# Standing pairs of TensorE transposes side by side in a two-block kernel: token halves, hidden tiles, exponentials, normed heads, diagonals

## The chip, the cores and the metric

One core of a Trainium2 chip runs the whole program in one launch. The metric is the time of the program on the device in microseconds (us). TensorE multiplies matrices and also does the transposes, as products with the identity; VectorE (DVE) and ScalarE (ACT) copy, scale and apply functions; GpSimd (POOL) does a few small things; SyncE (SP) issues the transfers of the weights.

## The reference

256 tokens of width 1024 pass through two blocks, each of two or one layers, in float32. Cut to what matters:

```
first block, layer 0 and layer 1:
  proj = rmsnorm(h) @ w_in[l];  main, mq = proj[..., :768], proj[..., 768:]
  main_out = pool_mixer(main)                       # layer 0
  main_out = swa_sink_attention(q(main), k, v)      # layer 1, 12 query heads, window 128
  mk, mv   = halves of rmsnorm(mem) @ w_mem_kv[l]
  mem_out  = softmax(norm(mq) @ norm(mk).T / 8) @ mv    # 4 heads of 64, 256 memory rows
  h += concat(main_out, mem_out) @ w_out[l]
  h += relu(rmsnorm(h) @ w_up[l])**2 @ w_down[l]
second block (normed h -> x):
  gated linear recurrence over the tokens (queries, forget gates, values per head of 128)
  block attention over normed query and key heads
  both, gated, through an output projection
  h += (silu(x @ w_gate) * (x @ w_up)) @ w_down
```

## The kernel before, in words

**Tiling.** The 256 tokens are two tiles of 128 (`tt` is 0 or 1). A left operand of a product needs its contraction axis on the partitions, so whatever is normed, gated or squared per token is first transposed: `tr` (line 159) multiplies one 128x128 piece by the identity `ident` into a PSUM bank called `mm`. Four such pieces fill a bank of 128x512, so transposes come in groups of four (two where a group has only two pieces), and one or two copies by ACT and DVE take a bank out.

**Precision.** A large product is three TensorE products of rounded halves: a weight is cast by ACT to `wh` (line 242) and its remainder is made by DVE as `wl` (line 243); an activation becomes `xh` and `xl` (`split`, lines 366 to 383), or `yh` and `yl` for a hidden tile. The three are (wh, xh), (wl, xh), (wh, xl), each 128x512 or 128x256 columns wide, at line 152. Weights come by SP's queue into `raw` tiles and go through eight buffers of `wh` and `wl`.

**Order.** A planner written out by hand (class `Line`, lines 88 to 121) sets the order of the program. Each piece of work is a generator task with a rank; it yields a delay in modelled us, or an event, when it has to wait for another engine. `mm` and `tr` move the planner's clock on. At each step the planner runs the task of the lowest rank whose delay has passed. So a `yield 1.3` between two groups of transposes lets other tasks (mostly the large products) issue in between. A list scheduler behind it then places instructions by engine; TensorE carries them out in the order that results.

**The places that the change touches.**

- `Norm.into` (line 401) normalizes a token tile, transposes its two halves of 512 columns (`xn`), and splits them; the two halves are apart by a `yield`. `turned` (line 508) does the same for a tile `h` that is not normed first.
- In `mlp` (line 553) `up_one` makes a hidden block for one token tile and hands it to `turn(b, tt, y)` (line 564), which transposes it (`hid`): four pieces in the square-relu MLPs, two in the gated one (class `SiluGate`, line 637). `up_one` is used for the blocks at the start of an MLP, before the steady loop.
- `mem_attention` (line 867) has two exponentials tiles `me`, one for each row half of the array; `exp_T` (line 441) transposes one into a bank and copies it as `eT` (ACT, line 448), and the products with the memory's values `mv` follow.
- `on_q` and `diagonal` (lines 1228 and 1240) make the diagonal of the recurrence's score matrix: many 32x32 products of `qs` and `fK` into an `mm` bank, and a multiplication by DVE into `AI` (line 1246). The recurrence then goes on in levels (line 1249), each with a burst of small products of `fQ` and `fK`.
- `heads_proj` and `heads_T` (lines 1385 and 1370) norm four heads of 128 (`hn`), transpose them and copy them out.

Of the kernel before, what the change touches and what calls it, by code (L numbers as in the profile page):

```python
# [15 lines left out]
P = 128  # L16
# [25 lines left out]
def kernel(  # L42
# [340 lines left out]
    class Norm:  # L383
# [17 lines left out]
        def into(self, xs, tt, g, done):  # L401

            xn, lat = self.xn, 1.2
            if self.r is None:
                self.rstd()
                lat = 3.0
            else:
                xn = keep.tile([P, D], F32, tag="xn", name="xn", bufs=2)
            for c in range(2):
                V.tensor_scalar(xn[:, half(c)], self.src[:, half(c)], self.r, None, op0=ALU.mult)  # L410
            for c in range(2):
                yield lat
                split_T(xn[:, half(c)], xs, tt, 4 * c, 4, g[:, 4 * c:4 * c + 4])
                lat = 0.8
            done.at(2.0)
# [92 lines left out]
    def turned(xs, src, tt, g, done):  # L508

        for c in range(2):  # L510
            split_T(src[:, half(c)], xs, tt, 4 * c, 4, None if g is None else g[:, 4 * c:4 * c + 4])
            yield 1.3
        done.at(1.5)

# [38 lines left out]
    def mlp(key, xs, there, nb, ku, hidden, finish, ends=1):  # L553
# [9 lines left out]

        def turn(b, tt, y):
            yield 3.2
            split_T(y, hT[b], tt, 0, ku)
            hT_there[b, tt].at(5.1)

        def up_one(b, tt):
# [4 lines left out]
            yield from lin(ps, ktiles(xs, tt), W((key, "up", b)))  # L574
            line.add(-2, turn(b, tt, hidden(ps)))

# [290 lines left out]
    def mem_attention(l, q, xs, tt, q_there, done):  # L867
# [20 lines left out]
        for i, ps in enumerate(pss):  # L888
# [9 lines left out]
            for hp in range(2):  # L898
                scaled(e[i][:, hp, :], sm[:, 2 * i + hp:2 * i + hp + 1])
        yield 3.2  # L900
        eTs = []
        for i in range(2):
            eTs.append(exp_T([e[i][:, hp, tok(c)] for hp in range(2) for c in range(2)]))
            yield 1.5
        po = by128(mm_bank())
# [313 lines left out]
    def on_f(c, hs, ps):  # L1219
        A.activation(fF[c][:, hs, :], ps, AF.Sigmoid)  # L1220
        A.activation(fK[c][:, hs, :], ps, AF.Sigmoid, scale=-1.0)
        for i in range(hs.start, hs.stop):
# [3 lines left out]
            V.tensor_scalar(k, k, olb[:, hd:hd + 1], None, op0=ALU.mult)  # L1226

    def on_q(c, hs, ps):
        V.scalar_tensor_tensor(fQ[c][:, hs, :], ps, HG_SCALE, fF[c][:, hs, :], op0=ALU.mult, op1=ALU.mult)
        qs = b2([2, S], "qs")  # L1230
        A.activation(qs, ps, AF.Copy, scale=HG_SCALE)
        line.add(5, diagonal(c, hs, qs))

# [5 lines left out]

    def diagonal(c, hs, qs):  # L1240
        yield 1.5
        pd = mm_bank()[:, :128].rearrange("p (h t) -> p h t", t=32)
        for i in range(2):
            for tt in range(TT):
                quarters(pd[:, 2 * i + tt, :], fK[c][:, hs.start + i, tok(tt)], qs[:, i, tok(tt)], 32)
        V.tensor_tensor(AI[c][:, 2 * hs.start:2 * hs.stop, :], pd, own[:, None, :].to_broadcast([P, 4, 32]), ALU.mult)
        diag_done[c, hs.start].at(2.1)

# [42 lines left out]

    diag_done = {(c, j): Event() for c in range(2) for j in (0, 2)}
    A_there, hv_there = events(), events()
# [7 lines left out]
    def recurrence(c):  # L1301
        yield [diag_done[c, 0], diag_done[c, 2]]
        for m in (1, 2, 4, 8, 16, 32, 64):
# [65 lines left out]

    def heads_T(t, dst, scale, done):  # L1370

        y = head_norm(t, 4, P, b2([4, P], "hn"))
        yield 8.4
        pt = by128(mm_bank())
        for i in range(4):
            tr(pt[:, i, :], y[:, i, :])
        if scale is None:
            A.copy(dst, pt)
        else:
            A.activation(dst, pt, AF.Copy, scale=scale)  # L1380
        left[done] = left.get(done, 0) + 1
        if left[done] == 2:
            done.at(5.8)

    def heads_proj(key, c, tt, dst, scale, done):
        t = b2([4, P], "tm")
        A.copy(t, by128((yield from project((key, c), x2, tt))))
        line.add(9, heads_T(t, dst, scale, done))

# [209 lines left out]
```

## Time and profile before

| | |
|---|---|
| median of 3 runs | 1031.24 us (1030.45 to 1032.26) |
| the profiled execution, its own time | 1031.49 us |
| its span, first to last instruction | 1029.6 us |
| TensorE products busy | 1022.1 us, 99% |
| TensorE weight loads (beside the products) | 901.6 us, 88% |
| VectorE busy | 640.0 us, 62% |
| ScalarE busy | 565.4 us, 55% |
| granted TensorE clock, mean | 1.000 |

The span is what the profile's pages divide into; the execution's own time is 1.9 us longer, and the median of the runs shown is 0.25 us below that execution's time. The rows of a timeline give the start, the length, the engine, the line, the operation and the tiles (out<-in). A product's end in the trace is modelled, and successive products overlap, so the cost of a group on TensorE is read from starts: from the start of the last product before it to the start of the second one behind it, less the usual distance of the products.

### The profile page before, as it was taken

The page shows a single profiled execution, that of the slowest core. Times are in us where ns is not written, and L with a number is a line of the kernel's source. Part 1 is how long each engine was busy: PE and PEld are TensorE (multiplying, and loading weights), DVE is VectorE, ACT ScalarE, POOL GpSimd, SP SyncE. Part 2 cuts the span into 40 slices and gives each one's busy share as a digit, 9 for nine tenths or more (in the row PEclk, how much of TensorE's full clock was granted, in tenths as well). Part 3 has the DMA queues.
Part 4 walks back from the last instruction along what each step waited for, and adds up shares of the span by engine and source line. Part 5 has one row for each costly group of instructions (what it writes and reads, how often), then busy time and mean ns, then how long its engine had stood idle before and what let it go on. Part 6 is the DMA issues. An engine that isn't in the chain of part 4 may idle for free.

```text
span 1029.6 us, 18411 instructions
## 1 busy us (share of the span) xinstructions
PE 1022.1 (99%) x7353; PEld 901.6 (88%) x7353; DVE 640.0 (62%) x1002; ACT 565.4 (55%) x904; POOL 100.8 (10%) x143
## 2 busy tenths in 40 slices
PE   9999999999999999999999999999999999999998
PEld 8768999998876788899988988888999988999997
DVE  6976664565678765564576569847635766455553
ACT  6856544454678654444466455758744455444341
POOL 1524000000142000000000004330000000000000
PEclk9999999999999999999999999999999999999999
DMA  9854566556552269666557554334455566565741
GB/s 339 279 164 163 166 196 208 169 185 207 181 165 82 71 182 327 198 191 212 171 181 237 196 165 165 124 124 156 142 184 175 179 196 199 164 216 167 231 145 41
DMA packets 107765, 186.40 MB, mean 181 GB/s; under 512 B 6808, under 2 KB 31648, under 8 KB 107680
## 3 DMA queue, kind: packets, MB, share of 16 engines
q1 hardware_dynamic: 106160, 180.13, 53.8%
q0 software_dynamic: 1104, 4.80, 1.4%
q8 instruction: 57, 0.93, 0.4%
q10 hardware_dynamic: 416, 0.30, 0.1%
q14 instruction: 28, 0.23, 0.1%
HBM read 182.58 MB, written 2.63 MB: 180 GB/s over the span
## 4 chain that ended last, share of the span: by engine, by line
PE 94%; DVE 2%; DMA 2%; issue 1%; ACT 0%; ACTq 0%
PE acc L152 58%; PE mm L152 33%; PE mm L159 3%; DMA raw<-in_w_mem_kv_dram 1%; DVE wl L248 1%; DMA raw<-in_w_in_dram 1%; DMA raw_T<-in_xT_dram 0%; DVE wl L243 0%; DVE u L932 0%; DVE u L820 0%; DVE hs L427 0%; ACT xn L398 0%; DVE win L931 0%; ACT wh L247 0%; DVE win L927 0%
## 5 line engine op out<-in xcount | busy, mean ns | idle before, releaser
L243 DVE TENSOR_TENSOR wl<-raw,wh 128x1024 fp32r<-128x1024 f32 (+1 forms) x316 | 378.2, 1219 | 174.0 <-ACT wh L242 168.2
L242 ACT CAST wh<-raw 128x1024 fp32r<-128x1024 f32 (+1 forms) x316 | 322.5, 1045 | 171.9 <-PE acc L152 100.0
L152 PE MATMUL mm<-xh,wh 128*128 128x256 f32 x752 | 208.2, 277 | 0.0
L152 PE MATMUL mm<-xl,wh 128*128 128x256 f32 x752 | 207.8, 276 | 0.0
L152 PE MATMUL mm<-xh,wl 128*128 128x256 f32 x752 | 207.7, 276 | 0.0
L152 PEld LDWEIGHTS mm<-xh,wh 128*128 128x128 f32 x752 | 141.2, 188 | 1.4 <-issue 0.4
L152 PEld LDWEIGHTS mm<-xl,wh 128*128 128x128 f32 x752 | 141.3, 188 | 1.0
L152 PEld LDWEIGHTS mm<-xh,wl 128*128 128x128 f32 x752 | 141.2, 188 | 0.0
L152 PE MATMUL acc<-wh,xh 128*128 128x512 f32 x336 | 138.1, 411 | 0.0
L152 PE MATMUL acc<-wh,yl 128*128 128x512 f32 x342 | 134.7, 394 | 0.0
L152 PE MATMUL acc<-wl,yh 128*128 128x512 f32 x342 | 134.0, 392 | 0.0
L152 PE MATMUL acc<-wh,yh 128*128 128x512 f32 x342 | 133.4, 390 | 0.0
L152 PE MATMUL acc<-wh,xl 128*128 128x512 f32 x337 | 132.5, 394 | 0.0
L152 PE MATMUL acc<-wl,xh 128*128 128x512 f32 x336 | 132.1, 393 | 0.0
L152 PE MATMUL acc<-xh,wh 128*128 128x256 f32 x416 | 115.6, 278 | 0.7 <-ACT wh L242 0.7
L152 PE MATMUL acc<-xh,wl 128*128 128x256 f32 x416 | 115.2, 277 | 0.5 <-DVE wl L243 0.5
L152 PE MATMUL acc<-xl,wh 128*128 128x256 f32 x416 | 115.2, 277 | 0.0
L152 PEld LDWEIGHTS acc<-xh,wh 128*128 128x128 f32 x416 | 78.1, 188 | 1.2 <-ACT wh L242 1.1
L152 PEld LDWEIGHTS acc<-xh,wl 128*128 128x128 f32 x416 | 78.1, 188 | 0.9 <-DVE wl L243 0.9
L152 PEld LDWEIGHTS acc<-xl,wh 128*128 128x128 f32 x416 | 78.2, 188 | 0.2
L152 PEld LDWEIGHTS acc<-wl,yh 128*128 128x128 f32 x342 | 64.2, 188 | 13.7
L152 PEld LDWEIGHTS acc<-wh,xh 128*128 128x128 f32 x336 | 63.2, 188 | 14.8 <-issue 2.8
(240 smaller groups left out, 1283.0 us busy)
## 6 DMA issues: line engine op xcount, KB each, us to landing
raw<-in_w_in_dram SPq DMA_DIRECT2D x86, 512.0 KB, 4.7
raw<-in_w_up_dram SPq DMA_DIRECT2D x64, 512.0 KB, 4.7
raw<-in_w_down_dram SPq DMA_DIRECT2D x64, 512.0 KB, 4.8
raw<-in_w_out_dram SPq DMA_DIRECT2D x24, 512.0 KB, 4.8
raw<-in_w_ffn_gate_dram SPq DMA_DIRECT2D x44, 256.0 KB, 4.2
raw<-in_w_ffn_up_dram SPq DMA_DIRECT2D x44, 256.0 KB, 4.6
raw<-in_w_ffn_down_dram SPq DMA_DIRECT2D x22, 512.0 KB, 5.2
raw<-in_w_mem_kv_dram SPq DMA_DIRECT2D x8, 512.0 KB, 10.3
```

The lines of the kernel that those rows point to most:

```text
L152: PE.matmul(out_, lhsT, rhs, start=start, stop=stop)
L159: PE.transpose(out_, in_, ident)
L242: A.copy(wh[:, ks, :], raw[:, ks, :])
L243: V.tensor_sub(wl[:, ks, :], raw[:, ks, :], wh[:, ks, :].bitcast(F32))
L248: V.scalar_tensor_tensor(wl[:, k, :], raw[:, k, :], gk, wh[:, k, :].bitcast(F32), op0=ALU.mult, op1=ALU.subtract)
```

## The change

Six places get their pairs put together:

1. `Norm.into`: for the first token tile there is one wait for both halves (the delay is the old one plus 0.8), and eight transposes in a row.
2. `turned`: for the first token tile both halves in a row; the event that says that the tile is there is given with 2.8 in place of 1.5.
3. `mlp`: hidden tiles of the first blocks are collected in a list, and two of them are turned by one task.
4. `mem_attention`: the wait ahead of the exponentials is 4.0 in place of 3.2, both are turned in a row, then there is one wait of 1.5.
5. `diagonal`: two head pairs go into one bank, and one DVE multiplication of 128x256 takes the place of two of 128x128.
6. `heads_proj`: the norm of a group of heads is made at once, and two groups are transposed by one task.

The diff (two edits of event names that follow from 5 are in it too):

```diff
--- before.py
+++ after.py
@@ -409,7 +409,9 @@
             for c in range(2):
                 V.tensor_scalar(xn[:, half(c)], self.src[:, half(c)], self.r, None, op0=ALU.mult)
             for c in range(2):
-                yield lat
+
+                if tt or c == 0:
+                    yield lat if tt else lat + 0.8
                 split_T(xn[:, half(c)], xs, tt, 4 * c, 4, g[:, 4 * c:4 * c + 4])
                 lat = 0.8
             done.at(2.0)
@@ -509,8 +511,9 @@
 
         for c in range(2):
             split_T(src[:, half(c)], xs, tt, 4 * c, 4, None if g is None else g[:, 4 * c:4 * c + 4])
-            yield 1.3
-        done.at(1.5)
+            if tt:
+                yield 1.3
+        done.at(2.8 if tt == 0 else 1.5)
 
     def add_turned(xs, g=None):
 
@@ -561,10 +564,13 @@
             for tt in range(TT):
                 hT_there[b, tt] = Event()
 
-        def turn(b, tt, y):
+        ys = []
+
+        def turn(ys):
             yield 3.2
-            split_T(y, hT[b], tt, 0, ku)
-            hT_there[b, tt].at(5.1)
+            for b, tt, y in ys:
+                split_T(y, hT[b], tt, 0, ku)
+                hT_there[b, tt].at(5.1)
 
         def up_one(b, tt):
 
@@ -572,7 +578,10 @@
                 hidden_tiles(b)
             ps = mm_bank()
             yield from lin(ps, ktiles(xs, tt), W((key, "up", b)))
-            line.add(-2, turn(b, tt, hidden(ps)))
+            ys.append((b, tt, hidden(ps)))
+            if len(ys) == 2:
+                line.add(-2, turn(ys[:]))
+                ys.clear()
 
         def up(b):
             hidden_tiles(b)
@@ -897,11 +906,11 @@
             V.reciprocal(sm[:, 2 * i:2 * i + 2], sm[:, 2 * i:2 * i + 2])
             for hp in range(2):
                 scaled(e[i][:, hp, :], sm[:, 2 * i + hp:2 * i + hp + 1])
-        yield 3.2
+        yield 4.0
         eTs = []
         for i in range(2):
             eTs.append(exp_T([e[i][:, hp, tok(c)] for hp in range(2) for c in range(2)]))
-            yield 1.5
+        yield 1.5
         po = by128(mm_bank())
         for hp in range(2):
             for c in range(2):
@@ -1225,11 +1234,16 @@
             V.tensor_scalar(f, f, olb[:, hd:hd + 1], lb[:, hd:hd + 1], op0=ALU.mult, op1=ALU.add)
             V.tensor_scalar(k, k, olb[:, hd:hd + 1], None, op0=ALU.mult)
 
+    qss = []
+
     def on_q(c, hs, ps):
         V.scalar_tensor_tensor(fQ[c][:, hs, :], ps, HG_SCALE, fF[c][:, hs, :], op0=ALU.mult, op1=ALU.mult)
         qs = b2([2, S], "qs")
         A.activation(qs, ps, AF.Copy, scale=HG_SCALE)
-        line.add(5, diagonal(c, hs, qs))
+        qss.append((hs, qs))
+        if len(qss) == 2:
+            line.add(5, diagonal(c, qss[:]))
+            qss.clear()
 
 
 
@@ -1237,14 +1251,15 @@
         for i in range(4):
             mm(ps[32 * i:32 * i + 32], keys[:, 32 * i:32 * i + 32], queries[:, n * i:n * i + n])
 
-    def diagonal(c, hs, qs):
+    def diagonal(c, qss):
         yield 1.5
-        pd = mm_bank()[:, :128].rearrange("p (h t) -> p h t", t=32)
-        for i in range(2):
-            for tt in range(TT):
-                quarters(pd[:, 2 * i + tt, :], fK[c][:, hs.start + i, tok(tt)], qs[:, i, tok(tt)], 32)
-        V.tensor_tensor(AI[c][:, 2 * hs.start:2 * hs.stop, :], pd, own[:, None, :].to_broadcast([P, 4, 32]), ALU.mult)
-        diag_done[c, hs.start].at(2.1)
+        pd = mm_bank()[:, :256].rearrange("p (h t) -> p h t", t=32)
+        for hs, qs in qss:
+            for i in range(hs.start, hs.stop):
+                for tt in range(TT):
+                    quarters(pd[:, 2 * i + tt, :], fK[c][:, i, tok(tt)], qs[:, i - hs.start, tok(tt)], 32)
+        V.tensor_tensor(AI[c], pd, own[:, None, :].to_broadcast([P, 8, 32]), ALU.mult)
+        diag_done[c].at(2.1)
 
     def level(m, c):
         def halves(t):
@@ -1289,7 +1304,7 @@
                 q = slice(32 * i, 32 * i + 32)
                 A.copy(at[q, :, q], AI[c][q])
 
-    diag_done = {(c, j): Event() for c in range(2) for j in (0, 2)}
+    diag_done = events()
     A_there, hv_there = events(), events()
 
     def gates_T(c):
@@ -1299,7 +1314,7 @@
         yield from head_chunk("hq", c, on_q)
 
     def recurrence(c):
-        yield [diag_done[c, 0], diag_done[c, 2]]
+        yield diag_done[c]
         for m in (1, 2, 4, 8, 16, 32, 64):
             level(m, c)
             yield 6.0
@@ -1367,25 +1382,30 @@
     q_there, k_there, v_there = events(), events(), events()
     left = {}
 
-    def heads_T(t, dst, scale, done):
-
-        y = head_norm(t, 4, P, b2([4, P], "hn"))
+    ys = []
+
+    def heads_T(ys, scale):
+
         yield 8.4
-        pt = by128(mm_bank())
-        for i in range(4):
-            tr(pt[:, i, :], y[:, i, :])
-        if scale is None:
-            A.copy(dst, pt)
-        else:
-            A.activation(dst, pt, AF.Copy, scale=scale)
-        left[done] = left.get(done, 0) + 1
-        if left[done] == 2:
-            done.at(5.8)
+        for y, dst, done in ys:
+            pt = by128(mm_bank())
+            for i in range(4):
+                tr(pt[:, i, :], y[:, i, :])
+            if scale is None:
+                A.copy(dst, pt)
+            else:
+                A.activation(dst, pt, AF.Copy, scale=scale)
+            left[done] = left.get(done, 0) + 1
+            if left[done] == 2:
+                done.at(5.8)
 
     def heads_proj(key, c, tt, dst, scale, done):
         t = b2([4, P], "tm")
         A.copy(t, by128((yield from project((key, c), x2, tt))))
-        line.add(9, heads_T(t, dst, scale, done))
+        ys.append((head_norm(t, 4, P, b2([4, P], "hn")), dst, done))
+        if len(ys) == 2:
+            line.add(9, heads_T(ys[:], scale))
+            ys.clear()
 
     def attention_in():
         for c in range(2):
```

Three places in TensorE's order, each before and then after. In all of them `acc<-wh,xh` and its like are pieces of large products.

In the recurrence, the level whose small products are 32x32 has two bursts of `fQ` (queries) and `fK` (keys). TensorE's order of before:

```order
L152 MATMUL acc<-wl,xh 128x512
L152 MATMUL acc<-wh,xl 128x512
L152 MATMUL mm<-fQ,fK 32x32 x16
L152 MATMUL acc<-wh,xh 128x512
L152 MATMUL acc<-wl,xh 128x512
L152 MATMUL acc<-wh,xl 128x512
L152 MATMUL acc<-wh,xh 128x512
L152 MATMUL acc<-wl,xh 128x512
L152 MATMUL acc<-wh,xl 128x512
L152 MATMUL mm<-fQ,fK 32x32 x16
L152 MATMUL acc<-wh,xh 128x512
L152 MATMUL acc<-wl,xh 128x512
```

And TensorE's order now:

```order
L152 MATMUL acc<-wh,xh 128x512
L152 MATMUL acc<-wl,xh 128x512
L152 MATMUL acc<-wh,xl 128x512
L152 MATMUL mm<-fQ,fK 32x32 x32
L152 MATMUL acc<-wh,xh 128x512
L152 MATMUL acc<-wl,xh 128x512
```

The two bursts, which had six large products between them, are one.

In the gated MLP's first blocks, TensorE's order of before around the second block's transposes of the second token tile (`hid` the hidden tile, `yh` and `yl` its split halves; the transposes of the first block's tile stand 12 large products earlier, in a group of two):

```order
L152 MATMUL acc<-wh,yh 128x512
L152 MATMUL acc<-wl,yh 128x512
L152 MATMUL acc<-wh,yl 128x512
L159 MATMUL mm<-ident,hid 128x128 x2
L152 MATMUL acc<-wh,yh 128x512
L152 MATMUL acc<-wl,yh 128x512
L152 MATMUL acc<-wh,yl 128x512
L152 MATMUL acc<-wh,yh 128x512
```

And TensorE's order now:

```order
L152 MATMUL acc<-wh,yh 128x512
L152 MATMUL acc<-wl,yh 128x512
L152 MATMUL acc<-wh,yl 128x512
L159 MATMUL mm<-ident,hid 128x128 x4
L152 MATMUL mm<-xh,wh 128x256
L152 MATMUL mm<-xl,wh 128x256
L152 MATMUL acc<-wh,yh 128x512
L152 MATMUL acc<-wl,yh 128x512
L152 MATMUL acc<-wh,yh 128x512
L152 MATMUL acc<-wh,yl 128x512
```

Both blocks' transposes now stand at the second's place, and the first block's tile is used three instructions later; it had 12 products between.

In layer 0's memory attention, TensorE's order of before where the second token tile's exponentials `me` are transposed and multiplied with the values `mv`:

```order
L152 MATMUL acc<-wh,xh 128x512
L152 MATMUL acc<-wl,xh 128x512
L152 MATMUL acc<-wh,xl 128x512
L152 MATMUL mm<-eT,mv_572 64x128 x7
L159 MATMUL mm<-ident,me 128x128 x4
L152 MATMUL mm<-eT,mv_572 64x128
L152 MATMUL acc<-wh,xh 128x512
L152 MATMUL acc<-wl,xh 128x512
L152 MATMUL acc<-wh,xl 128x512
L152 MATMUL mm<-eT,mv_572 64x128 x7
```

And TensorE's order now:

```order
L152 MATMUL acc<-wh,xh 128x512
L152 MATMUL mm<-eT,mv_572 64x128
L159 MATMUL mm<-ident,me 128x128 x2
L152 MATMUL mm<-eT,mv_572 64x128 x7
L159 MATMUL mm<-ident,me 128x128 x6
L152 MATMUL acc<-wl,xh 128x512
L152 MATMUL acc<-wh,xl 128x512
L152 MATMUL mm<-eT,mv_572 64x128
L152 MATMUL acc<-wh,xh 128x512
L152 MATMUL mm<-eT,mv_572 64x128 x7
```

The eight transposes of the second tile stand around one group of products, and between them and the tile's own products there are two large ones and then one more; before, one tile's second group of four stood directly ahead of its first product with the values, with three large products behind that.

## Rows read from the trace of the kernel before

**Rows 1.** The page's busy times and shares by engine.

```profile
PE 1022.1 (99%) x7353; PEld 901.6 (88%) x7353; DVE 640.0 (62%) x1002; ACT 565.4 (55%) x904; POOL 100.8 (10%) x143
```

**Rows 2.** The page's chain of work that ended last, by engine.

```profile
PE 94%; DVE 2%; DMA 2%; issue 1%; ACT 0%; ACTq 0%
```

**Rows 3.** TensorE's waits, first and last of six: cause; us, times, longest.

```profile
PE mm L159 <- POOL ks L435: 1.1, 1, 1.1
...
PE mm L152 <- DVE u L932: 0.2, 1, 0.2
```

**Rows 4.** TensorE's timeline around one group of four: start, us, operation, tiles, count.

```profile
84.33 0.40 PE L152 MATMUL acc<-wh,xl 128*128 128x512 f32 x1
84.56 0.60 PE L159 MATMUL mm<-ident,h 128*128 128x128 f32 x4
...
85.23 0.40 PE L152 MATMUL acc<-wl,xh 128*128 128x512 f32 x1
```

**Rows 5.** TensorE's timeline around one group of eight.

```profile
776.64 0.28 PE L152 MATMUL acc<-xh,wl 128*128 128x256 f32 x1
776.76 1.03 PE L159 MATMUL mm<-ident,ho 128*128 128x128 f32 x8
...
777.75 0.28 PE L152 MATMUL acc<-xl,wh 128*128 128x256 f32 x1
```

**Rows 6.** TensorE's timeline, one of the two 32x32 bursts of the recurrence.

```profile
650.48 0.40 PE L152 MATMUL acc<-wh,xl 128*128 128x512 f32 x1
650.81 1.10 PE L152 MATMUL mm<-fQ,fK 128*32 128x32 f32 x32
651.83 0.50 PE L152 MATMUL acc<-wh,xh 128*128 128x512 f32 x1
652.17 0.39 PE L152 MATMUL acc<-wl,xh 128*128 128x512 f32 x1
```

**Rows 7.** TensorE's timeline, transposes directly behind a small burst.

```profile
344.71 0.66 PE L152 MATMUL mm<-eT,sv 128*64 128x128 f32 x8
345.30 0.66 PE L159 MATMUL mm<-ident,sc 128*128 128x128 f32 x4
345.71 0.47 PE L152 MATMUL acc<-wh,xh 128*128 128x512 f32 x1
346.02 0.39 PE L152 MATMUL acc<-wl,xh 128*128 128x512 f32 x1
```

**Rows 8.** All engines' timeline, the gated MLP's first blocks.

```profile
869.75 1.23 DVE L243 TENSOR_TENSOR wl<-raw,wh 128x1024 fp32r<-128x1024 f32 x1 [0.35 <-ACT wh L242]
869.92 0.38 PE L159 MATMUL mm<-ident,hid 128*128 128x128 f32 x2
870.34 0.37 ACT L370 CAST yh<-mm 128x256 fp32r<-128x256 f32 x1 [0.63 <-PE mm L159]
870.89 0.42 DVE L371 TENSOR_TENSOR yl<-mm,yh 128x256 fp32r<-128x256 f32 x1
```

**Rows 9.** All engines' timeline, layer 0's memory attention.

```profile
68.68 1.04 ACT L242 CAST wh<-raw 128x1024 fp32r<-128x1024 f32 x1
...
70.17 0.56 ACT L895 ACTIVATE me<-acc,ms,mr 128x256 f32<-128x256 f32 x1
...
70.72 1.07 ACT L448 COPY eT<-mm 128x512 f32<-128x512 f32 x2
71.39 1.09 PE L152 MATMUL mm<-eT,mv 128*64 128x128 f32 x14
...
73.10 0.59 ACT L448 COPY eT<-mm 128x512 f32<-128x512 f32 x1 [0.21 <-PE mm L159]
```

**Rows 10.** All instructions of the diagonal's multiplication: ns least, median, most; first, last.

```profile
L1246 DVE TENSOR_TENSOR AI<-mm,own x4: 281/281/284, 609.3 to 609.9; 128x128 f32<-128x128 f32 x4
```

**Rows 11.** Busy us by engine in two stretches, clock, DMA share, GB/s.

```profile
316.00:352.00 36.00, 36.00 (x253) 25.25 (x252) 24.84 (x91) 25.67 (x76) 5.68 (x28) 1.00 0.10 30
606.00:640.00 34.00, 33.47 (x759) 27.14 (x758) 30.46 (x49) 15.72 (x21) 10.49 (x8) 1.00 0.47 154
```

## The prediction

> **What bounds the kernel now.** I read the page's busy times first. TensorE has 1022.1 us of products in a span of 1029.6, and VectorE and ScalarE are at 62% and 55% [rows 1]. The chain of work that ended last says the same from the other end: TensorE 94%, and the "issue" share, time in which it waited for nothing that shows, 1% [rows 2]. The waits of TensorE come to six entries, the largest 1.1 us and the smallest 0.2 [rows 3], so at most 6.6 us can be had from waits of any kind, and the two rows shown name small instructions of layer 0's mixing (`ks` on GpSimd, `u` on VectorE). The reader is to see that the time is the sum of TensorE's instructions. A change can then win only where an instruction itself gets cheaper or an empty place between two goes, and it loses only where TensorE is made to wait.
>
> The instructions are the same in number and size: the order shows the same 5791 large products before and after, the same transposes, and the same weight transfers in the same order on SP's queue; GpSimd's order differs in three small copies. What changes on TensorE is the number of groups of other work that stand within the large products, 97 before and 81 now, and the changes of kind between neighbours (transposes, small products, large products), 239 before and 205 now. So the price of a group is what has to be read.
>
> **The change part by part.**
>
> *What a group of transposes costs for being apart.* A group of four in the stream of 512-column products: the product ahead starts at 84.33, the second one behind at 85.23, and the usual distance of such products is 0.23 (84.33 to 84.56), so the group takes 0.90 - 2 x 0.23 = 0.44, or 0.110 per transpose [rows 4]. A group of eight in the stream of 256-column products: 776.64 to 777.75 is 1.11, less two distances of 0.12 (776.64 to 776.76), which leaves 0.87, or 0.109 per transpose [rows 5]. Two groups of four cost 0.88, one of eight 0.87: a merge of full-size transposes is worth about 0.01. Of the 16 groups that go, 15 are such or lie beside other small work: 15 x 0.01 = -0.15. The bounds from these two rows are 0 and 15 x 0.03 (the rounding of three starts), 0 to -0.45.
>
> *The two 32x32 bursts of the recurrence become one.* Their entry is 650.48 to 650.81, 0.33, and the exit 651.83 to 652.17, 0.34; against 0.23 a burst pays 0.10 and 0.11, together 0.21 [rows 6]. One entry and one exit go: -0.2. If the 1.02 between 650.81 and 651.83 held a fixed part as well, more would go; by half of it -0.7, the far bound.
>
> *Normed heads.* Eight groups of four become four of eight (counted above), and two of these stand directly behind a burst. The nearest rows are other transposes behind a small burst: the transposes start at 345.30, the large product at 345.71 and its successor at 346.02, so four transposes and their exit take 0.41 + 0.31 - 0.23 = 0.49, and the burst's own exit of 0.11 [rows 6] isn't paid: 0.38 against 0.44 apart [rows 4, 7]. Two such places: -0.1 (0 to -0.2).
>
> *Diagonals.* TensorE already does all of them in one stretch, so nothing goes there. VectorE makes two multiplications of twice the width in place of four of 0.281 each [rows 10]: at most 0.56 less, on an engine that is busy 30.46 of 34 us there while TensorE is at 33.47 [rows 11]. Off the path, taken as 0; a bound is -0.5, the part that TensorE is idle in that stretch.
>
> *Halves of the first token tile, and the MLPs' hidden tiles with four pieces.* The first half's transposes move back to the second half's. The first products that use either tile stay where they were in the stream of large products; the nearest is 18 products behind the merged group, 18 x 0.23 = 4.1 us [rows 4], and a copy and its remainder, as 0.37 and 0.42 in another place [rows 8], are far shorter. Two banks need two of each: 1.6 in all. Hidden; without that cover it would be 1.6 each.
>
> *The gated MLP's first blocks.* Here the cover goes. The first block's transposes of the second tile had 12 large products behind them; now they stand at 869.92 beside the second block's and the first use is three instructions on. TensorE does four transposes, 0.44, and two 256-column products, 0.23, until 870.59. The cast `yh` started at 870.34 after such a pair and took 0.37, so until 870.71; TensorE waits 0.12. Then it has two products (0.46), and needs `yl`, whose subtraction waits on VectorE behind a weight's remainder (869.75, 1.23, until 870.98) and takes 0.42 [rows 8]: it is there at 871.4, TensorE is at about 871.2. The sum is 0.12 + 0.2 = +0.3. Behind the waiting products on TensorE stand only products of the same block, and nothing else waits for them. From below it is 0.1 (the cast alone), from above 1.3 (a whole remainder of 1.23 comes between).
>
> *Memory exponentials.* A pair of transposed groups now needs two copies of ACT in a row, 1.07 for both and 0.59 for one; before, one tile's second copy ran at 73.10 beside three large products, and the products with the values started at 71.39 just as ACT was done with the copies begun at 70.72 [rows 9]. Now there are three large products, 0.69, between the last transposes and the seven products that need the second copy. 1.07 - 0.69 is 0.38 short if ACT copies both only after the last transpose; the first two transposes stand earlier, so the first copy may run beside the others; I take 0.25 for each of layer 0's two tiles: +0.5. Layer 1's tiles lie in a stretch where TensorE is at 36.00 of 36 and ACT at 25.67 [rows 11], with other work to hand: 0. Bounds: 0, and a cast of 1.04 [rows 9] ahead of the copies in both, 2 x (1.07 + 1.04 - 0.69) = +2.8.
>
> **The sum.** -0.15 - 0.2 - 0.1 + 0.3 + 0.5 = +0.35, rounded +0.3. The profiled execution took 1031.49, 0.25 above the median of the runs, 1031.24; so 1031.8 for an execution like it and 1031.5 for a median. The bounds added up go from about -1.8 to +4.
>
> Here the trace can be weighed against a rule. A small burst pays 0.10 going in and 0.11 coming out [rows 6], a full-size transpose group next to nothing [rows 4]. The Trainium skill, page "TensorEngine Tiling (Array Packing)", section "Key Properties", says that a change of tiling mode (and not merely of the tile) drains the engine. By that rule the merged bursts win, and the whole-array transposes, which change no tiling, win nothing; the trace agrees, with its 0.21 for a burst.
>
> **Rivals.**
>
> *Every change of kind empties the array.* If going from a large product to a transpose cost what going to a small burst costs, each of the 34 changes that go would be worth 0.10 [rows 6]: -3.4, with the two waits above about -2.6, and 1031.24 - 2.6 makes 1028.6; without the waits 1027.8. For it: the bursts do pay it, and some of the 34 lie at bursts. Against it: the group of four shows 0.44 for four transposes with both of its edges in it [rows 4].
>
> *ACT becomes the engine that the memory attention waits for.* Place: the two copies of each of the four tiles, two in each layer. Price: the second copy, 0.59, in full for each of the four, and a cast of 1.04 ahead of one or two of them [rows 9], which the scheduler may put there: 4 x 0.59 + 1.04 to 2.08 = 3.4 to 4.4, less 0.45 gained and with the 0.3 of the gated MLP: about +3.3 to +4.3, 1034.5 to 1035.5; without any cast ahead 1033.5. It decides from the point at which the large products between transposes and use are shorter than what ACT has to do. For it: they are 0.69 against 1.07 in layer 0. Against it: in layer 1 ACT has 10 us in 36 to spare [rows 11].
>
> *The pairs don't come together where it matters.* The recurrence's stretch keeps its order but for the places named, and the diagonals stood together: nothing but +-0.3, inside the forecast's range.
>
> **How the numbers follow.** A measurement of this kernel can tell about 0.2% from no change, 2.06 us: 1029.18 and 1033.30 are the marks. The forecast, 1031.5 with its waits between nothing and twice what I take (1029.8 to 1033.0), has 0.75. The slower rival has 0.15, the faster 0.10. So faster 0.10, same 0.75, slower 0.15. The range of 1029.4 to 1033.6 holds the forecast's own and the lower end of the slower rival; it leaves out the faster one and most of what the slower one would give with casts ahead.
>
> **What would show it.** In the profile after, TensorE's groups of eight transposes should cost 0.87 by the same reading of starts, and the one 32x32 burst should have one entry of 0.33 and one exit of 0.34 around some 2.0. At the gated MLP's merged group there should be two gaps, behind the cast and behind the remainder, of 0.1 to 0.2. In layer 0's memory attention the products with the values should wait for the copies `eT`, some 0.2 for a tile; waits of 0.6 and more at all four tiles would make the slower rival right. A TensorE busy time lower by 2 us or more with the same instructions would make the faster one right, and my reading of the edges wrong.

## The result

The changed kernel takes 1039.43 us (median of 4 runs, 1037.79 to 1039.98) against 1031.57 for the kernel before (4 runs, 1030.45 to 1032.26); the ratio is 1.006, 95% interval 1.0035 to 1.0084. It is slower by about 8 us, far outside the predicted 1029.4 to 1033.6. Timed runs of one kernel differ in their mean granted clock, and with it by some us (before, in one later series, from 1030.62 us at 0.999 to 1036.87 at 0.995), so what a place costs is read from the starts in the profiles.

The page's busy line of the change, which answers to [rows 1], and the two largest of TensorE's waits, which answer to [rows 3] (engine, line, cause; us in total, times, longest):

```profile
PE 1028.2 (99%) x7353; PEld 909.2 (88%) x7353; DVE 640.6 (62%) x1000; ACT 565.6 (54%) x904; POOL 103.0 (10%) x143
```

```profile
PE mm L152 <- ACT eT L450: 1.9, 1, 1.9
PE mm L159 <- POOL ks L437: 1.1, 1, 1.1
```

TensorE has the same 7353 products and is busy 6.1 us longer, and there is one new wait of more than 0.2 us. To see where the time goes, I compared the start of each large product; their order is the same in both programs but for ten in the gated MLP's first blocks. The lag of the change (how much later the same product starts than in before) grows or falls in a few places and is nearly flat in between (the ends of the stretches lie where no group has changed its place):

| stretch (time in the trace before) | lag gained, first profile | second profile |
|---|---|---|
| 104 to 262, first MLP's loop | +2.74 | +2.74 |
| 300 to 354, layer 1's mixing | +3.89 | +2.36 |
| 545 to 608, second block's projections | +1.66 | +1.66 |
| 608 to 615, first burst of the recurrence | +0.07 | +0.65 |
| 615 to 690, the rest of the recurrence | -0.60 | -0.60 |
| 690 to 740 | +0.34 | +0.03 |
| 850 to 873.6, gated MLP's first blocks | +0.22 | +0.22 |
| 873.6 to the end | +0.50 | +0.50 |

The second profile is of the change run once more (below). Up to 104 it stays within some 0.5 us, but for groups that changed places, and differs between executions. In the first burst of the recurrence every profile has a wait, of differing length, for nothing that the profile shows ("issue": 0.5 in the profile before, 0.6 and 1.2 in the two of the change). The first MLP's loop, the second block's projections and the last stretch have no wait at all. The busy times of a stretch that holds nothing but back-to-back 256-column products (columns: from:to in us, length, then busy us and number of instructions of PE, PEld, DVE, ACT, POOL; granted clock, DMA share, GB/s) show what is slower there. In before:

```profile
575.00:600.00 25.00, 25.00 (x223) 25.00 (x223) 15.52 (x24) 11.31 (x15) 0.00 (x0) 1.00 0.64 215
```

and in the change:

```profile
575.00:600.00 25.00, 25.00 (x214) 25.00 (x213) 13.35 (x20) 11.51 (x15) 0.00 (x0) 1.00 0.51 171
```

The engine is busy in full and the granted clock is 1.00 in both, and yet 214 products fit where 223 did. From their starts one product takes 113.3 ns in before and 117.8 in the change. The 512-column products keep 229 ns in both.

The rows for the layer 1 wait, all engines' timeline of the change:

```profile
332.25 0.56 ACT L904 ACTIVATE me<-acc,ms,mr 128x256 f32<-128x256 f32 x1 [2.36 <-DVE ms L900]
332.54 0.39 PE L152 MATMUL acc<-wh,xl 128*128 128x512 f32 x1
...
333.89 0.56 ACT L904 ACTIVATE me<-acc,ms,mr 128x256 f32<-128x256 f32 x1
...
334.43 0.86 ACT L450 COPY eT<-mm 128x256 f32<-128x256 f32 x2
...
334.86 0.44 PE L152 MATMUL mm<-eT,sv 128*64 128x128 f32 x4 [1.93 <-ACT eT L450]
```

ScalarE does the four memory exponentials `me` from 332.25 to 334.4, and only then the copy `eT` of the window attention, for which TensorE stands still 1.93 us with nothing else ahead of it. ScalarE isn't short of time here: ahead of the first exponential it stands idle for 2.36 us, until VectorE has made `ms`, and VectorE does a weight's remainder first. What the copy reads was transposed at 329.90, four microseconds before the copy:

```profile
329.90 0.44 PE L159 MATMUL mm<-ident,sc 128*128 128x128 f32 x2
...
330.24 1.22 DVE L243 TENSOR_TENSOR wl<-raw,wh 128x1024 fp32r<-128x1024 f32 x1
...
331.37 0.79 DVE L900 TENSOR_TENSOR ms<-ms,mr 128x2 f32<-128x2 f32 x1
```

In before the copies that TensorE needs there stand ahead of the exponentials:

```profile
328.05 0.59 ACT L448 COPY eT<-mm 128x512 f32<-128x512 f32 x1
...
331.17 0.56 ACT L895 ACTIVATE me<-acc,ms,mr 128x256 f32<-128x256 f32 x1 [0.88 <-DVE ms L891]
```

The stretches from the wait on, in the change:

```profile
332.00:334.00 2.00, 0.93 (x5) 0.42 (x3) 1.44 (x5) 1.75 (x7) 1.93 (x22) 1.00 0.66 166
334.00:336.00 2.00, 1.14 (x8) 0.64 (x10) 1.59 (x7) 1.77 (x5) 0.00 (x0) 0.79 0.26 97
336.00:338.00 2.00, 2.00 (x13) 1.67 (x14) 0.88 (x2) 0.98 (x2) 0.00 (x0) 0.50 0.03 8
338.00:340.00 2.00, 2.00 (x12) 1.45 (x11) 0.53 (x4) 1.23 (x3) 0.00 (x0) 0.86 0.00 0
```

After the wait the granted clock falls to 0.50, the lower of its two levels (1.2 GHz), and is back by 340. That makes the difference between +3.89 here and +2.36 in the second profile, where the wait is the same 1.9 and the clock stays at 1.00: the wait belongs to the program, the low clock behind it only to some executions.

The terms of the prediction's sum can be read too. A group of eight in the 512-column stream, answering to [rows 4, 5]:

```profile
83.95 0.40 PE L152 MATMUL acc<-wh,xl 128*128 128x512 f32 x1
84.19 1.03 PE L159 MATMUL mm<-ident,h 128*128 128x128 f32 x8
84.97 0.48 PE L152 MATMUL acc<-wh,xh 128*128 128x512 f32 x1
85.29 0.39 PE L152 MATMUL acc<-wl,xh 128*128 128x512 f32 x1
```

83.95 to 85.29 less two distances of 0.23 is 0.88: two of four apart cost 0.88 as well. The one burst of the 32x32 level, answering to [rows 6]:

```profile
661.04 0.40 PE L152 MATMUL acc<-wh,xl 128*128 128x512 f32 x1
661.37 1.91 PE L152 MATMUL mm<-fQ,fK 128*32 128x32 f32 x64
663.21 0.50 PE L152 MATMUL acc<-wh,xh 128*128 128x512 f32 x1
663.55 0.39 PE L152 MATMUL acc<-wl,xh 128*128 128x512 f32 x1
```

2.51 less 0.46 is 2.05, against 2 x 1.23 before: -0.41. Entry and exit are 0.33 and 0.34, as in one burst before; the other 0.20 lies between them, where the 64 products take 1.84 and not 2 x 1.02. The gated MLP's merged group, answering to [rows 8]:

```profile
877.31 0.60 PE L159 MATMUL mm<-ident,hid 128*128 128x128 f32 x4
...
877.87 0.28 PE L152 MATMUL mm<-xl,wh 128*128 128x256 f32 x1
...
878.15 0.50 PE L152 MATMUL acc<-wh,yh 128*128 128x512 f32 x1
878.48 0.39 PE L152 MATMUL acc<-wl,yh 128*128 128x512 f32 x1
```

The wait for the cast is the step from 877.87 to 878.15, 0.28 where the distance is 0.12. The forecast wait for the remainder `yl` isn't there: the next steps are 0.33 and 0.23. Layer 0's memory attention costs nothing: the lag is 0.1 us smaller behind it than ahead of it.

### The profile page after: what moved, and what is told of

It reads as the page before. It is cut to its first block, busy times and chain, and to the rows that moved or that the text cites. A ratio compares the mean times of both kernels' runs of the same rounds, so it can differ in the third digit from the quotient of the medians.

```text
span 1037.9 us, 18411 instructions
## 1 busy us (share of the span) xinstructions
PE 1028.2 (99%) x7353; PEld 909.2 (88%) x7353; DVE 640.6 (62%) x1000; ACT 565.6 (54%) x904; POOL 103.0 (10%) x143
## 4 chain that ended last, share of the span: by engine, by line
PE 93%; DMA 3%; DVE 2%; issue 1%; ACT 0%; SPq 0%; ACTq 0%; DVEq 0%
PE acc L152 58%; PE mm L152 32%; PE mm L159 3%; DMA raw<-in_w_mem_kv_dram 1%; DVE wl L248 1%; DMA h<-in_x_dram 1%; DMA raw<-in_w_in_dram 1%; DMA raw_T<-in_xT_dram 0%; DVE u L941 0%; DVE wl L243 0%; ACT me L904 0%; DVE hs L429 0%; DVE win L940 0%; ACT L1512 0%; DVE sc L454 0%
## 5 line engine op out<-in xcount | busy, mean ns | idle before, releaser
L152 PEld LDWEIGHTS acc<-wh,yh 128*128 128x128 f32 x342 | 64.2, 188 | 13.6 <-ACT yh L370 0.2
L152 PEld LDWEIGHTS acc<-wh,yl 128*128 128x128 f32 x342 | 64.4, 188 | 13.3
```

What stands on the lines that cost most here:

```text
L152: PE.matmul(out_, lhsT, rhs, start=start, stop=stop)
```

## The experiments

**The same two programs again.** Is the slow pace part of the program, or of the execution? No edit.

> The whole change, run once more. Read from the first profile, 8.4 us are lost at two kinds of places: 3.9 around layer 1's mixing (a wait of 1.9 for the copy eT, then about 4 us in which the granted clock is as low as 0.50), and some 5 where back-to-back 256-column products start 117.8 ns apart and not 113.3, which one execution shows in some stretches and not in others. Theory A: the wait belongs to the program, so it comes again at the same place with the same length (1.9 +- 0.3) and a clock of 0.5 behind it. Theory B, on the pace: it belongs to the program too, and the slow stretches (104 to 262, 568 to 750) come again; its rival: the pace is set anew in each execution, and the slow stretches lie elsewhere or are of another length. By B 1038 to 1040 us, by the rival 1035 to 1042.

> The kernel before, run once more, for a second profile of it. By theory B the 256-column products stand at 113.3 ns nearly everywhere, as in its first profile (117.8 only at 720 to 727); by the rival, long stretches at 117.8 appear in it as well. 1030.5 to 1032.3 us by B; up to 1036 by the rival. No wait over 0.3 us in layer 1's mixing by either.

Measured: 1039.16 and 1030.55 us. The change has 214 products in 575 to 600 again, before 223. The wait of 1.9 came again; the clock of 0.5 did not. So theory A holds for the wait and not for the clock. Theory B holds for the long stretches; in two places the pace changed from one execution to the next: in the first 25 us, where both paces appear in either program, and at 719 to 732 of the change, where some 70 products stand 117.8 ns apart in the first profile and 113.3 in the second (the +0.34 and +0.03 of the table).

**The memory exponentials, without and alone.** The first is the change with `mem_attention` as before, the second the kernel before with this edit:

```diff
-        yield 3.2
+        yield 4.0
         eTs = []
         for i in range(2):
             eTs.append(exp_T(...))
-            yield 1.5
+        yield 1.5
```

> The whole change but for the memory exponentials (mem_attention as before). Theory A: the wait for eT at layer 1's mixing and the low clock behind it go, 3.9 us less than the change: 1035.5 (+- 0.8). Rival: the wait comes from another part, for example from the tiles' halves that now come together ahead of it, and stays: 1039.5. The slow pace is not touched by theory A; if it goes as well, the time is near 1031.

> The memory exponentials' edit alone, on the kernel before. Theory A: 3.5 to 4 us over before, 1035.2, with the wait of about 1.9 us and the clock at 0.5 behind it. Rival: the wait comes only where other parts shift the window attention too, and this is 1031.6 +- 0.7. If the pace belongs to what is merged elsewhere, all 256-column stretches stand at 113.3 here.

Measured: without it 1036.17 us, 1.0038 of before (1.0021 to 1.0055); alone 1034.96, 1.0029 (1.0016 to 1.0043). Without it the lag of 300 to 354 is 0.00 and the slow stretches stay (+2.74 and +1.66); alone it is +2.43 and the 256-column stretches of both MLPs and of the second block are fast. Theory A is right on the place, and each of the two costs comes without the other.

**Its two halves.** The pairing with the old delay of 3.2, and the delay of 4.0 with the groups apart.

> The memory exponentials turned in pairs, with the planner's old delay of 3.2 in place of 4.0, on the kernel before. Theory A1: the wait of 1.9 us in layer 1's mixing comes from the longer delay, which puts the four exponentials on ScalarE ahead of the window attention's copy eT; here it goes, and this is 1031.8 +- 0.8. Rival A2: it comes from the two groups in a row (no other work between), and stays: 1035.

> The planner's delay of 4.0 alone, the exponentials turned apart as before. A1: the wait of 1.9 us and the low clock behind it are here, 1035. A2: no such wait, 1031.8.

Measured: 1032.54 us, 1.0016 (1.0004 to 1.0027), and 1032.90, 1.0026 (1.0013 to 1.0039). Neither has the wait of 1.9: their largest new waits are 0.5 each (the second also has 1.2 for `u` in layer 0, where before has 1.1 for `ks`; that comes in kernels with other edits too). A1 and A2 both fall for that wait: it comes only with the pair and the longer delay together. With the delay alone the copies stand ahead of the exponentials, as in before. With the pair alone they stand behind them, as in the change, but eleven large products lie on TensorE between the copy's transposes (329.96) and the products that need the copy (334.18), where the change has six, and the wait for `eT` is 0.2. The time is another matter: from the end of the first MLP to the end of the mixing they lag by 1.4 and 1.1, where both together lag 2.4, so each half costs its part without the long wait. The intervals of the three overlap, so by time alone they are not told apart.

**Hidden tiles and token halves, alone.** The edits are parts 3, and 1 with 2, of the diff; the last is the change without part 3.

> The MLPs' edit alone (hidden tiles turned in pairs), on the kernel before. The slow pace of the 256-column products came in the same stretches in both profiles of the change and without the memory edit, and in none of before, so it belongs to the program. Theory B1: it follows a merged group of transposes close ahead; in the change it begins at 112, directly behind the merged hidden tiles. Then this alone has 117.8 ns from 112 to 262 and at 881 to 891 and 113.3 at 568 to 720: +2.6 to +3.1 us over before, less nothing, with the small waits of 0.3 at the gated MLP. Rival B2: the pace hangs on the halves of the token tile (turned, Norm.into) merged earlier; then this is +0.3 (+-0.5), all at 113.3.

> The halves of the first token tile alone (Norm.into and turned), on the kernel before. By theory B1 the stretch 568 to 720, which comes behind merged xn tiles, is at 117.8 ns here and the first MLP at 113.3: +2 us. By B2 both are slow: +4.8. By a third view, that a slow stretch needs both parts, nothing: 0 +- 0.5.

> The whole change but for the hidden tiles. By B1 the first MLP is at 113.3 ns, 568 to 720 stays slow: 8.3 - 3 = +5 us over before, some 1036.5, with the wait of 1.9 us in layer 1's mixing. By B2 the first MLP stays slow: +8.

Measured: 1036.59 us, 1.004 (1.0025 to 1.0055); 1033.31, 1.0013 (1.0002 to 1.0024); 1037.76, 1.0051 (1.0035 to 1.0067). By lag the last costs 2.7 (that execution took 1034.16 us, at a clock of 1.000; the other five were at 0.994 to 0.998). The first MLP is slow with the hidden tiles merged (+2.74) and fast without. The second block's stretch is slow with either edit: in the hidden tiles' kernel nothing near it is merged, the last merge lies some 180 us ahead. And the second MLP, whose hidden tiles are merged in the same way directly ahead of its loop, keeps the fast pace in every profile with such a merge (median 113 ns). So B1 is right on the first MLP and wrong in its "close ahead"; B2 is wrong.

**One transpose more, up to three.** A piece is transposed again into the same place, once to three times, at the second tile's group in the first MLP, with and without the merge:

```diff
-        for i in range(n):
+        for i in [0] * more + list(range(n)):
             tr(pt[:, i, :], src[:, i * P:(i + 1) * P])
```

> The kernel before with one transpose done twice: the second token tile's group of hidden tiles in the first MLP is five in place of four (one piece is written twice to the same place). Nothing is merged and TensorE's order is otherwise the same. Phase theory: the large products run in a beat of three (starts 226, 229, 232 ns apart in the fast stretches, 229, 232, 226 in the slow ones), the beat is carried from one stretch to the next, and any work of another length put between shifts it; a merge is only one such shift. Then 0.11 us more work can put the first MLP on the slow pace: +2.9 us with 117.8 ns from 113 to 262. Rival: merging itself (eight transposes and more in a row) makes the slow pace; then this is +0.1 us, all at 113.3.

> The MLPs' edit alone with the same one transpose more (nine in place of eight in the first MLP). Phase theory: the shift is another one, and the first MLP may be fast again (113.3 ns from 113 to 262; about -2.5 us against the edit alone, 1034) though more is merged than before. Rival (merging makes it): slow as with eight, 1036.7.

> The kernel before with six transposes in place of four at the second hidden tile of the first MLP (two pieces more, written to the same places as before). Phase theory: the pace of the 256-column products behind depends on where in the beat of three the large products resume, so in the series of 4, 5, 6, 7 transposes (no merge) and 8, 9, 10, 11 (merged) both paces occur on either side; 4 and 5 are fast, 8 slow and 9 fast so far. Rival: the slow pace needs the merge (eight in a row, with the first group gone from its place), and 6 and 7 are fast. A slow first MLP here gives 4.4 ns per product from 113 to 262, 1034.3 us; a fast one 1031.9.

> As the one before, with seven transposes. Phase theory: slow in one of six and seven, 1034.4; rival: fast in both, 1032.

> The MLPs' edit alone with ten transposes in place of eight. Both views say fast or slow here by the phase; if the number of transposes sets it with a period, as 8 slow and 9 fast suggest, ten is fast and eleven slow (a period of three). Slow 1036.8, fast 1034.6.

> The MLPs' edit alone with eleven transposes: slow by a period of three in the number of transposes (1036.9), fast if nothing recurs (1034.7).

Measured: 1031.71, 1034.59, 1031.67, 1032.35, 1036.61 and 1035.77 us (the last four one run each, beside one of before of 1030.50). The lag gained from 113 to 247, most of the first MLP's loop, against before (8 is the hidden tiles' kernel):

| transposes | 4 | 5 | 6 | 7 | 8 merged | 9 merged | 10 merged | 11 merged |
|---|---|---|---|---|---|---|---|---|
| lag, us | 0 | 0.00 | -0.01 | +0.41 | +2.59 | +0.01 | +2.59 | 0.00 |

One more transpose, more work and more of it in a row, takes the slow pace of the merge away in this loop (the second block's stretch stays slow in all four merged kernels): the nine cost 1.0027 of before (1.0014 to 1.0039) where the eight cost 1.0040. The same stretch with the eight, and then with the nine, counts 70 and 73 products (before 73):

```profile
131.00:139.00 8.00, 8.00 (x70) 8.00 (x69) 2.21 (x3) 1.64 (x3) 0.00 (x0) 1.00 0.58 188
```

```profile
131.00:139.00 8.00, 8.00 (x73) 8.00 (x72) 2.31 (x3) 1.86 (x3) 0.00 (x0) 1.00 0.59 192
```

And seven without any merge are slow for one section of 48 256-column products, directly behind the group (44 from 113.5 to 118.5, before 46), and fast from the next such section on (from 131). Between these lie 48 512-column products that are slow as well, 233 ns apart and not 229; each section makes half of the +0.41:

```profile
113.50:118.50 5.00, 5.00 (x44) 5.00 (x44) 2.33 (x4) 2.73 (x4) 0.00 (x0) 1.00 0.03 10
131.00:139.00 8.00, 8.00 (x73) 8.00 (x72) 2.95 (x4) 1.69 (x3) 0.00 (x0) 1.00 0.67 228
```

```profile
L152 PE MATMUL acc<-wh,yh 128*128 128x512 f32 x16 | 6.4, 398 | 0.0
```

So the rival (only the merge brings it) falls; the number of transposes has no period of three either, since ten are slow and eleven fast. The trace shows a mark of the state. In the next 512-column section of the loop, 142 to 151, the mean lengths of the three kinds of product are, in before (columns: line, engine, operation, tiles, shape, count; busy us, mean ns; idle time before, as in the row of the seven above, which is from 119 to 130):

```profile
L152 PE MATMUL acc<-wh,yl 128*128 128x512 f32 x14 | 5.5, 394 | 0.0
L152 PE MATMUL acc<-wh,yh 128*128 128x512 f32 x14 | 5.4, 388 | 0.0
L152 PE MATMUL acc<-wl,yh 128*128 128x512 f32 x13 | 5.1, 392 | 0.0
```

and in the change:

```profile
L152 PE MATMUL acc<-wl,yh 128*128 128x512 f32 x14 | 5.5, 394 | 0.0
L152 PE MATMUL acc<-wh,yl 128*128 128x512 f32 x14 | 5.4, 388 | 0.0
L152 PE MATMUL acc<-wh,yh 128*128 128x512 f32 x13 | 5.1, 392 | 0.0
```

The lengths 388, 392, 394 go round in that order in both, and the distances of the starts, which are not modelled, with them (226, 229, 232 ns), but they begin at another product of the triple. In the first MLP's loop this shift goes with the slow pace: before, five, six, nine and eleven transposes have the order of before and are fast, eight and ten have that of the change and are slow. Once there, order and pace last to the end of the loop, through sections of 11 us of either width; with seven, both changed once more across the slow 512-column section. The shift is a mark in its place and no rule by itself: in the 512-column products ahead of the second block's projections it also splits all twenty profiles, but there the products behind are fast with 388 at the third product of the triple and slow with 388 at the first, where in the first MLP 388 at the first is fast and at the third slow. What sets it, and why the pace of the 256-column products goes with it (4.4 ns for each), no run here settled.

**Heads and diagonals.** Parts 5 and 6 alone, twice, and part 6 alone.

> Normed heads and diagonals alone, on the kernel before. In the change the stretch of the recurrence (616 to 690) gains 0.6 us over before by the aligned starts of the large products; so -0.6 by theory, with the 256-column products as in before, since the merges come behind nearly all of that stretch's 256-column work; +1 if it puts the products of 700 to 750 on the slow pace.

> Normed heads and diagonals alone once more, in more rounds: the first time it was 0.999 of before. Its trace has all the 256-column products on the fast pace that before has there, no wait in layer 1's mixing, and 0.56 us less from 625 to 681. If that is the gain: 0.9992 to 0.9995 of before; if the first ratio was chance, 1.000.

> Normed heads alone. The diagonals' edit moves nothing on TensorE, so the gain is the heads' (among it the two 32x32 bursts, which come together once the heads' groups stand elsewhere): the same as with the diagonals, 0.9992 to 0.9995 of before. If the halved VectorE work counts: 0.2 us more than with the diagonals.

Measured: 1030.59 us, 0.9990 of before (0.9981 to 0.9999); 1031.23, 0.9986 (0.9975 to 0.9996); heads alone 1030.86, 0.9988 (0.9973 to 1.0003). The two parts that leave the slow pace out make a version that is faster than the kernel before, by 1.2 and 1.1 us in the medians, and by 0.8 and 0.7 where the mean clock was 0.999 or more. The heads' own interval holds 1, and the three don't differ among themselves, so whether the halved VectorE work counts is open. The profiles show where the gain sits, once the "issue" wait of the first burst, which differs in every execution, is left out: from 615 to 690 the lag falls by 0.5 to 0.6 in all six profiles of kernels with both parts, and lies between -0.05 and +0.8 in the twelve others that have neither. From 690 to 740 it falls by another 0.3 in both profiles of this version, where the slow stretch of before at 721 to 725 is gone. The profiled execution of the heads alone says nothing on the edit: its "issue" wait was 2.6 us, and behind it the granted clock stood at 0.50 from 618 to 622, which cost 4.3 together.

## Why the prediction was wrong, point by point

- *"The time is the sum of TensorE's instructions", and these are the same.* This is the step that failed. They are the same, but I took an instruction's price as fixed. The price of the 256-column products, 0.12 in [rows 5], is one of two, 113.3 and 117.8 ns, and the change puts the first MLP's loop, the second block's projections and the gated MLP's first section on the dearer one: 2.74 + 1.66 + 0.50 = 4.9 us of 8. I had looked for the cost of a merge inside the merged group, where it is nothing, and not in what comes behind. No rival had it: the faster one priced changes of kind, the other waits. What sets the pace stays open.
- *Layer 1's memory exponentials: 0, "with other work to hand".* Wrong, the second failure: +2.36, and +3.89 with the low clock. ScalarE's total was indeed low in that stretch (25.67 of 36, [rows 11]), but a total says nothing on the order in which its queue stands: the copy came last while ScalarE was idle. The rival on ScalarE had the engine right, and its price was for the copies of all four tiles; what came is one wait, for another task's copy behind four exponentials. It gave 1033.5 to 1035.5.
- *Layer 0's memory exponentials: +0.5.* Measured -0.1: nothing.
- *The gated MLP: +0.3.* Measured +0.22, with the wait for the cast where it was put, 0.16 against 0.12. The 0.2 for `yl` did not come: the weight's remainder that was to stand ahead of it on VectorE (876.18, 1.22) was done before the cast. That the sum comes out near is in part luck.
- *Groups of transposes: 0.01 a merge.* Right: 0.88 for eight.
- *The two 32x32 bursts: -0.2.* Right in kind, -0.41 measured between the same products: the 0.21 of one entry and exit, and 0.20 inside the burst, which lies within the bound that the prediction gave for a fixed part.
- *Heads, diagonals: -0.1 and 0.* Right in sign: with the bursts, which come together in the same edit, -0.3 was forecast; the profiles show -0.6 in the recurrence, the timed runs -0.7 to -1.2.
- *Token halves and four-piece hidden tiles: hidden.* Their copies are; the pace is what they cost.
- *The rule that a change of tiling mode drains the engine* (the Trainium skill, page "TensorEngine Tiling (Array Packing)", section "Key Properties", as the prediction cites it). The trace agrees as far as it goes: one burst less saved 0.41, twice the 0.21 of [rows 6], and merged transposes of full size nothing (0.88 for eight). That it is a drain is not shown by any run here.

What could have been seen ahead of time: the page of before gives 277 ns and 1.00 of the clock for these products and no hint of a second pace, but its trace has one. At 721 to 725 thirty 256-column products stand 117.8 ns apart, behind a group of small ones. An unexplained stretch of other pace in the stream that bounds a kernel should have been a rival with a price: some 620 products in the loop by 4.4 ns is 2.7 us.

## What to carry to other kernels

In a kernel whose one engine is always busy, compare the starts of the same instruction in two traces before looking for waits: more than half of this loss lay in stretches without any. A term may be hidden in what an inserted group does to the stream behind it, so an edit to such a stream is measured part by part, and the parts that leave the pace alone are kept. And where a task's delay in a planner is changed, ask on each engine's queue which other task's work now stands behind it, since a low share of busy time doesn't answer that: the copy here waited behind exponentials that an idle ScalarE could not yet start.

## What the hardware showed that I had not expected

- Two paces of back-to-back 256-column products at the same granted clock of 1.00, 113.3 and 117.8 ns, kept over tens of us, with the 512-column products at 229 ns in both, but for one section at 233 (seven transposes). Within a program the long stretches are the same in each profile; two executions of one program differ in the first 25 us (15 to 22: 64 products in the first profile of before, 61 in its second) and, in the change, at 719 to 732.
- A wait of 1.9 us was followed by a granted clock of 0.50 in one execution of the change and not in another; that cost 1.5 us, nearly as much as the wait. In the profile of the heads alone a wait of 2.6 us was followed by 0.50 as well.
